# The second norm of a hybrid layer: early MLP weights split inside the output projection's sweep, and scaled stream differences

## The chip, the core and the metric

The kernel runs on one core of one Trainium2 chip. The metric is device time in microseconds (us) from the start to the end of one execution. The engines are named as in the profile: PE (TensorE, the matmuls), PEld (its weight loads), DVE (VectorE), ACT (ScalarE), POOL (GpSimd) and SP (SyncE, which issues the DMAs here).

## The reference, cut to what matters

One layer: a normed and modulated input goes through attention and gated linear attention, the two are merged, projected and added to `x`; then a second norm, a modulation and an MLP with a squared ReLU, added again. The change lies where the first residual becomes the second norm's input.

```
def rms_norm(x, g):
    y = x * lax.rsqrt(jnp.mean(x * x, axis=-1, keepdims=True) + EPS)
    return y * g
def modulate(h, shift, scale):
    return h * (1 + scale) + shift
def sq_relu_mlp(h, w1, w2):
    return jnp.square(jax.nn.relu(h @ w1)) @ w2
# in hybrid_layer
    x = x + gt1 * ((...) @ w_out)                       # branch_merge ends with w_out
    x = x + gt2 * sq_relu_mlp(modulate(rms_norm(x, norm2), sh2, sc2), w_mlp1, w_mlp2)
```

Sizes: 1024 tokens, `D_MODEL` 1024, `D_FF` 4096, all float32.

## The kernel before

The stream is kept transposed: 128 channels on the partitions, tokens along the free axis. `th` is a half of the tokens (512 columns), `c` a half of the channels. Every product is three matmuls (`mm3`, lines 163 to 165): the float32 operands are split into a high part (a cast on ACT) and a low part (a subtraction on DVE), and high x high, high x low and low x high are summed. A weight block is split by `split` (lines 1111 and 1112) into one of six buffers tagged `W`; an activation block by `split_block` (lines 1138 and 1139). A **product** below is one `product` call: twelve matmuls of 512 columns.

`out_projection` multiplies by `w_out`. For each `th` and `c` it loads two 1 MB weight tiles (`R`, two buffers), makes eight products into four PSUM banks, adds the residual on DVE (line 1300), stores the new stream to `x` in DRAM (line 1301, on SP's queue) and squares it on ACT (1306) to sum the squares on DVE (1307). After each `th` the sum goes over the partitions by eight small matmuls (line 350), a reciprocal root is made on DVE (lines 121 to 126), transposed to all partitions by PE (line 362) and copied by ACT (1328). Then every tile of the half is multiplied by the root (DVE 1333), and scaled and shifted on ACT (1334).

The MLP's first matrix is multiplied by a seven-product scheme: `unit(u)` makes a 1024 x 256 slice of it with seven products instead of eight, in the order `(0, 1, 5, 4, 6, 2, 3)`. Their right sides are blocks `B[i, j]`, four tiles `j` each: blocks 0 and 1 are the first token half, 5, 4, 6, 2 and 3 are sums and differences that need the second half. Their weights are, likewise, plain blocks (0, 1, 3) or sums that `sums` makes on POOL (lines 1159 to 1162) for 5, 4, 6 and 2. `sink` takes the products out of PSUM (lines 1379 to 1414), squares them and stores them to `u`. There are 16 units, run in pairs.

Since blocks 0 and 1 need the first half alone, units 0 to 3 run their products 0 and 1 (eight in all) behind the output projection, and `norm2_second` makes the other five blocks meanwhile: on DVE two multiplications by the root, two differences and five low parts for each of four tile pairs `j` (36 instructions), on POOL eight subtractions, on ACT the scale and shift and the casts. `mlp` then goes on with units 0 and 1.

The code gives an order of issue; a scheduler places the instructions of each engine by it and by its own estimate of time, and each engine runs its list in that order. `tc.issue_after` puts instructions behind another one. SP issues DMAs in order, and a DMA waits there until its buffer is free.

## Time and profile before

| | |
|---|---|
| time, median of 3 runs | 2125.89 us (2125.73 to 2126.91) |
| time of the profiled execution | 2125.22 us, of which the span of instructions 2123.5 us |
| PE busy | 2014.4 us (95%) |
| DVE busy | 1435.5 us (68%) |
| ACT busy | 1053.7 us (50%) |
| POOL busy | 677.7 us (32%) |
| mean granted TensorE clock | 0.984 of full speed |
| chain that ended last | PE 75%, DVE 11%, ACT 4%, DMA 4% |

An engine's busy time says how much work it has; where the time goes is read from the waits of PE, stretch by stretch, and from the instructions on the other engines that stand behind each wait.

### The profile page before, as it was taken

The page shows a single profiled execution, that of the slowest core. Times are in us where ns is not written, and L with a number is a line of the kernel's source. Part 1 is how long each engine was busy: PE and PEld are TensorE (multiplying, and loading weights), DVE is VectorE, ACT ScalarE, POOL GpSimd, SP SyncE. Part 2 cuts the span into 40 slices and gives each one's busy share as a digit, 9 for nine tenths or more (in the row PEclk, how much of TensorE's full clock was granted, in tenths as well). Part 3 has the DMA queues.
Part 4 walks back from the last instruction along what each step waited for, and adds up shares of the span by engine and source line. Part 5 has one row for each costly group of instructions (what it writes and reads, how often), then busy time and mean ns, then how long its engine had stood idle before and what let it go on. Part 6 is the DMA issues. An engine that isn't in the chain of part 4 may idle for free.

```text
span 2123.5 us, 32583 instructions
## 1 busy us (share of the span) xinstructions
PE 2014.4 (95%) x12526; PEld 1682.6 (79%) x12526; DVE 1435.5 (68%) x2088; ACT 1053.7 (50%) x1833; POOL 677.7 (32%) x436
## 2 busy tenths in 40 slices
PE   4999998999999999899999898999699999999999
PEld 2888777898889999677788686877588888788887
DVE  6533766749484387778777678857756457798794
ACT  3344655455553232687766543445555556344341
POOL 2100231322222022362301456103433235475470
PEclk9999999999999999999999999999899999999999
DMA  8234320212223333872311476744154547645441
GB/s 290 68 105 128 106 61 27 86 37 60 78 64 95 107 127 123 289 238 85 95 50 46 153 237 202 259 170 149 43 176 148 180 144 243 224 144 163 135 154 65
DMA packets 217339, 284.12 MB, mean 134 GB/s; under 512 B 18864, under 2 KB 139840, under 8 KB 217184
## 3 DMA queue, kind: packets, MB, share of 16 engines
q1 hardware_dynamic: 217120, 281.90, 40.6%
q8 instruction: 99, 1.62, 0.3%
q0 software_dynamic: 64, 0.13, 0.1%
q14 instruction: 56, 0.46, 0.1%
HBM read 200.18 MB, written 81.81 MB: 133 GB/s over the span
## 4 chain that ended last, share of the span: by engine, by line
PE 75%; DVE 11%; ACT 4%; DMA 4%; issue 3%; POOL 2%; SPq 1%; ACTq 0%; DVEq 0%; POOLq 0%
PE g L163 12%; PE g L165 12%; PE g L164 12%; PE p L165 8%; PE p L163 8%; PE p L164 7%; PE b L986 2%; PE a L713 1%; DVE G L863 1%; PE b L163 1%; PE b L165 1%; PE b L164 1%; PE s L163 1%; DMA S<-in_w_ada_dram 1%; PE a L715 1%
## 5 line engine op out<-in xcount | busy, mean ns | idle before, releaser
L163 PE MATMUL g<-whi,S 128*128 128x256 f32 x896 | 259.2, 289 | 0.0
L165 PE MATMUL g<-whi,S 128*128 128x256 f32 x896 | 251.2, 280 | 0.0
L164 PE MATMUL g<-wlo,S 128*128 128x256 f32 x896 | 250.5, 280 | 0.0
L1112 DVE TENSOR_TENSOR W<-Q,W 128x512 fp32r<-128x512 f32 x160 | 132.1, 830 | 103.6 <-ACT W L1111 103.1
L163 PE MATMUL p<-S,W 128*128 128x512 f32 x384 | 155.8, 406 | 22.6 <-ACT W L1111 19.0
L163 PEld LDWEIGHTS g<-whi,S 128*128 128x128 f32 x896 | 169.1, 189 | 1.8
L164 PEld LDWEIGHTS g<-wlo,S 128*128 128x128 f32 x896 | 169.1, 189 | 1.1
L165 PEld LDWEIGHTS g<-whi,S 128*128 128x128 f32 x896 | 169.1, 189 | 0.0
L1111 ACT CAST W<-R 128x512 fp32r<-128x512 f32 x152 | 93.9, 619 | 150.3 <-PE p L165 104.7
L1159 POOL TENSOR_TENSOR Q<-R 128x512 f32<-128x512 f32 x40 | 60.2, 1504 | 310.5 <-DVE W L1112 215.7
L163 PE MATMUL g<-S,whi 128*128 128x512 f32 x368 | 151.9, 413 | 5.8 <-ACT S L258 5.8
L165 PE MATMUL p<-S,W 128*128 128x512 f32 x384 | 155.4, 405 | 1.8 <-DVE W L1112 1.8
L151 POOL TENSOR_TENSOR wlo<-wraw,whi 128x1024 fp32r<-128x1024 f32 x32 | 81.8, 2571 | 234.7 <-ACT whi L150 218.9
L1112 DVE TENSOR_TENSOR W<-R,W 128x512 fp32r<-128x512 f32 x152 | 140.5, 926 | 21.8 <-ACT W L1111 21.8
L164 PE MATMUL p<-S,W 128*128 128x512 f32 x384 | 155.1, 404 | 0.0
L1111 ACT CAST W<-Q 128x512 fp32r<-128x512 f32 x160 | 98.4, 621 | 109.0 <-PE g L165 52.0
L164 PE MATMUL p<-G,W 128*128 128x512 f32 x384 | 152.0, 396 | 0.0
L165 PE MATMUL p<-G,W 128*128 128x512 f32 x384 | 151.9, 395 | 0.0
L163 PE MATMUL p<-G,W 128*128 128x512 f32 x384 | 151.9, 395 | 0.0
L164 PE MATMUL g<-S,whi 128*128 128x512 f32 x368 | 147.1, 400 | 0.0
L165 PE MATMUL g<-S,wlo 128*128 128x512 f32 x368 | 146.8, 399 | 0.0
L181 DVE TENSOR_TENSOR G<-b,G 128x512 fp32r<-128x512 f32 x160 | 108.9, 686 | 42.3 <-ACT G L180 41.7
(332 smaller groups left out, 5511.8 us busy)
## 6 DMA issues: line engine op xcount, KB each, us to landing
R<-in_w_mlp_dram SPq DMA_DIRECT2D x32, 1024.0 KB, 6.0
wraw<-in_w_in_dram SPq DMA_DIRECT2D x60, 512.0 KB, 3.9
u<-S SPq DMA_DIRECT2D x96, 256.0 KB, 2.3
S<-in_w_ada_dram SPq DMA_DIRECT2D x32, 512.0 KB, 5.9
G<-u SPq DMA_DIRECT2D x64, 256.0 KB, 3.6
S<-u SPq DMA_DIRECT2D x48, 256.0 KB, 3.5
G<-in_w_ada_dram SPq DMA_DIRECT2D x16, 512.0 KB, 10.6
R<-in_w_out_dram SPq DMA_DIRECT2D x8, 1024.0 KB, 6.2
```

The costliest lines, as they stand in the source:

```text
L151: self.lo_engine.tensor_tensor(lo[:, s, :], raw, hi[:, s, :].bitcast(F32), op=ALU.subtract)
L163: nc.tensor.matmul(out, lh, rh, start=first, stop=False, skip_group_check=more)
L164: nc.tensor.matmul(out, lh, rl, start=False, stop=False, skip_group_check=more)
L165: nc.tensor.matmul(out, ll, rh, start=False, stop=last, skip_group_check=more)
L181: self.nc.vector.tensor_tensor(lo, src, hi.bitcast(F32), op=ALU.subtract)
L713: nc.tensor.matmul(po, qd[:, s], sb, start=d == 1, stop=True)
L715: nc.tensor.matmul(pu, kd[:, s], vt(c), start=True, stop=True)
L863: nc.vector.tensor_tensor(uv[:, :, :, s, :], xv[:, :, :, 1 - s, :], tv[:, :, :, s, :], op=ALU.mult)
L986: nc.tensor.transpose(pt[:, h * P:(h + 1) * P], src, self.ident)
L1111: self.nc.scalar.copy(hi, v)
L1112: self.nc.vector.tensor_tensor(lo, v, hi.bitcast(F32), op=ALU.subtract)
L1159: tt(s[0], a21, a22, op=ALU.add)
```

## The change

The change rewrites what lies between the second half of the output projection (`th` = 1) and the MLP's units.

- Units 0 and 1 get their weights in the sweep: `early_weights` loads each unit's 1 MB in two tiles of the pool `S` (rows of 1 KB), before the sweep of `th` = 1 instead of behind it, and their `sums` on POOL are traced there. Units 2 and 3 get `half_weights`: 512 KB with rows of 512 B, for products 0 and 1 alone; their whole 1 MB is loaded again later. `ahead` splits six weight blocks between the last products of the projection: (unit 0, product 0), (1, 0), (0, 1), (1, 1), (2, 0), (3, 0).
- In the sweep ACT scales the even tiles of the stream in place by `mc[:, 2]` (line 1349), and DVE makes the scaled difference of odd and even tile, `t2` (line 1351), before the root is known. Behind the root a tile pair needs a multiplication and an addition for block 5, a multiplication and a scalar_tensor_tensor (STT) for block 4, and so on: with the low parts 44 instructions on DVE, none on POOL. The root is read from PSUM, without ACT's copy. The first half's even tiles get the shift's difference `dsh` added on ACT (four instructions) at the end of `norm2_first`.
- `norm2_second` yields after each block, and units 0 and 1 take their products in between.

```
@@ mm3, product
-        nc.tensor.matmul(out, ll, rh, start=False, stop=last, skip_group_check=more)
+        return nc.tensor.matmul(out, ll, rh, start=False, stop=last, skip_group_check=more)
+            if j == 1:
+                self.last_mm = r
@@ unit
+            if i == 5 and early is not None:
+                if "sums" in w:
+                    self.rest(blk, A, w, w.pop("sums"))
+                else:
+                    raw = self.raw_weights(src)
+                    self.rest(blk, A, w)
+                yield
...
+    def early_weights(self, u):
+        raw = [self.S(F32, (P, 4, 256)) for _ in range(2)]
+        for e in range(2):
+            self.nc.sync.dma_start(raw[e], self.wcols("w_mlp1", u * 256)[:, e::2, :])
+        return lambda kh, s: raw[kh][:, :, s * P:(s + 1) * P]
+    def half_weights(self, u):
+        raw = self.S(F32, (P, KT, P))
+        self.nc.sync.dma_start(raw, self.wcols("w_mlp1", u * 256)[:, :, 0:P])
+        return lambda kh, s: raw[:, kh::2, :]
@@ out_projection
+            if th == 1:
+                blk = [(self.half_weights if u > 1 else self.early_weights)(u) for u in range(4)]
+                early = [{"blk": blk[u], "sums": self.sums(blk[u])} for u in range(2)] + [{}, {}]
+                t2 = [self.S(F32, (P, 2, 512)) for _ in range(2)]
+                def ahead(u, i):
+                    early[u][i] = self.split(blk[u](i, 0))
...
+                    if th and c and kh:
+                        ahead(0, 0)
+                        ahead(1, 0)
...
+                        if th:
+                            j, e = b // 2, Z[1, 0, c][:, i // 2, :]
+                            if b % 2 == 0:
+                                nc.scalar.mul(e, e, mc[:, 2, b:b + 1])
+                            else:
+                                nc.vector.scalar_tensor_tensor(t2[c][:, i // 2, :], v, mc[:, 2, b:b + 1], e, op0=ALU.mult, op1=ALU.subtract)
+                        if th and c:
+                            ahead(*((0, 1), (1, 1), (2, 0), (3, 0))[i])
...
-        for u in (0, 1, 0, 1, 2, 3, 2, 3):
-            next(units[u])
-        self.norm2_second(rb, z)
+        rs, after = self.token_rstd(ssq)
+        next(units[0])
+        with self.tc.issue_after(after.ins):
+            next(units[1])
+        with self.tc.issue_after(self.last_mm.ins):
+            rp, _ = self.on_all(rs)
+        ahead(2, 1)
+        ahead(3, 1)
+        with self.tc.issue_after(after.ins):
+            next(units[0])
+        for u in (1, 2, 3, 2, 3, 0, 1):
+            next(units[u])
+        for _ in self.norm2_second(rp[0], z, lambda j: t2[j // 2][:, j % 2, :]):
+            for u in (0, 1):
+                next(units[u])
@@ norm2_second (new body)
+        for j in range(4):
+            tt(u(j), u(j), rb, op=ALU.mult)
+            tt(z(1, 1, j), u(j), z(0, 0, j), op=ALU.add)
+            self.block(5, j, z(1, 1, j))
+        yield
+        for j in range(4):
+            tt(z(1, 0, j), z(1, 0, j), rb, op=ALU.mult)
+            stt(z(0, 0, j), z(1, 0, j), sh(j), z(0, 0, j), op0=ALU.add, op1=ALU.subtract)
+            self.block(4, j, z(0, 0, j))
+        yield
+        for j in range(4):
+            b = self.B[6, j] = self.four(6)
+            nc.scalar.activation(b[:, 0, :], u(j), AF.Identity, bias=dsh(j))
+            stt(b[:, 1, :], u(j), dsh(j), b[:, 0, :].bitcast(F32), op0=ALU.add, op1=ALU.subtract)
+        yield
+        for j in range(4):
+            stt(u(j), u(j), sh(j), z(1, 0, j), op0=ALU.add, op1=ALU.add)
+            self.block(2, j, u(j))
+        yield
+        for j in range(4):
+            tt(u(j), z(0, 1, j), z(1, 1, j), op=ALU.subtract)
+        for j in range(4):
+            self.block(3, j, u(j))
+        yield
```

The order of the instructions, at three places. ACT at the end of the sweep, before: squares of the stream (`m<-G`) and casts of MLP weights (`W<-R`) alternate, and the last square (L1306) is followed by a copy out of PSUM.

```order
L1306 ACTIVATE m_14019<-G_13910 128x512 [waits DVE_49,Activation_49]
L1111 CAST W_14157<-R_14109 128x512 [waits PE_49,Activation_49]
L1306 ACTIVATE m_14039<-G_13908 128x512 [waits DVE_49,Activation_49]
L1111 CAST W_14178<-R_14109 128x512 [waits PE_49]
L1306 ACTIVATE m_14059<-G_13910 128x512 [waits DVE_49,Activation_49]
L1391 COPY S_14107<-p_14094 128x512 [waits PE_49]
L1111 CAST W_14187<-R_14185 128x512 [waits DMAHW4_49]
L1328 COPY m_14087<-a_14082 128x512 [waits PE_49,Activation_49]
```

ACT there now: before the last square (L1343, fourth from the end) stand two scalings of the stream in place (L1349) and three weight casts, one of them of the projection's last block (`W_14094`).

```order
L1343 ACTIVATE m_14039<-G_13942 128x512 [waits DVE_49]
L1111 CAST W_14091<-S_13770 128x512 [waits DMAHW0_49,PE_49,Activation_49]
L1349 ACTIVATE G_13942<-G_13942,mc 128x512 [waits DMAHW7_49,Activation_49]
L1343 ACTIVATE m_14063<-G_13944 128x512 [waits DVE_49]
L1111 CAST W_14094<-R_14014 128x512 [waits PE_49]
L1343 ACTIVATE m_14087<-G_13942 128x512 [waits DVE_49]
L1349 ACTIVATE G_13942<-G_13942,mc 128x512 [waits DMAHW1_49,Activation_49]
L1111 CAST W_14115<-S_13772 128x512 [waits DVE_49,PE_49]
L1343 ACTIVATE m_14111<-G_13944 128x512 [waits DVE_49]
L1453 COPY S_14151<-p_14138 128x512 [waits PE_49]
```

Two of these instructions wait for a DMA (`DMAHW`): the scalings, until the store of the unscaled tile has left. The last square now stands behind them.

PE, at the last product of unit 0 (product 3, into `p_14094`), before: it stands behind both units' product 2 (`g_14428` is unit 1's) and waits for nothing there.

```order
L163 MATMUL g_14428<-G_14356,W_14505 128x512
L164 MATMUL g_14428<-G_14356,W_14505 128x512
L165 MATMUL g_14428<-G_14356,W_14505 128x512
L163 MATMUL p_14094<-G_14363,W_14150 128x512
L164 MATMUL p_14094<-G_14363,W_14150 128x512
L165 MATMUL p_14094<-G_14363,W_14150 128x512
L163 MATMUL p_14094<-G_14366,W_14150 128x512
```

PE there now (unit 0's product 3 goes into `p_14138`, `p_14213` is unit 2's product 5, `g_14376` unit 1's product 2):

```order
L163 MATMUL p_14138<-G_14509,W_14277 128x512 [waits Activation_49]
L164 MATMUL p_14138<-G_14509,W_14277 128x512 [waits DVE_49]
L165 MATMUL p_14138<-G_14509,W_14277 128x512
L163 MATMUL p_14138<-G_14512,W_14277 128x512 [waits Activation_49]
L163 MATMUL p_14213<-S_14285,W_14577 128x512 [waits Activation_49]
L164 MATMUL p_14138<-G_14512,W_14277 128x512 [waits DVE_49]
L165 MATMUL p_14138<-G_14512,W_14277 128x512
L163 MATMUL p_14138<-G_14515,W_14277 128x512
L164 MATMUL p_14138<-G_14515,W_14277 128x512 [waits DVE_49]
L163 MATMUL g_14376<-G_14442,W_14481 128x512 [waits Activation_49]
```

Unit 0's product 3 moved ahead of unit 1's product 2, waits for casts and low parts tile by tile, and one matmul of unit 2, whose weights are POOL's sum, stands within it.

DVE at the end of the norm's work, before: the four low parts of block 3 (`G_14363` to `G_14372`), then the weight splits of units 0 and 1.

```order
L1139 TENSOR_TENSOR G_14363<-S_14281,G_14363 128x512 [waits Activation_49]
L1139 TENSOR_TENSOR G_14366<-S_14281,G_14366 128x512 [waits Activation_49]
L1139 TENSOR_TENSOR G_14369<-S_14282,G_14369 128x512 [waits Activation_49]
L1139 TENSOR_TENSOR G_14372<-S_14282,G_14372 128x512 [waits Activation_49]
L1112 TENSOR_TENSOR W_14375<-Q_14145,W_14375 128x512
L1112 TENSOR_TENSOR W_14391<-Q_14173,W_14391 128x512
L1112 TENSOR_TENSOR W_14407<-Q_14145,W_14407 128x512 [waits PE_49,Activation_49]
L1112 TENSOR_TENSOR W_14425<-Q_14173,W_14425 128x512 [waits PE_49,Activation_49]
```

DVE there now: a weight split of each of units 0 and 1 (`W_14457`, `W_14481`: product 2), four differences (L1424) and the low parts of block 3.

```order
L1441 TENSOR_TENSOR S_14371<-S_14371,p_14138 128x512 [waits PE_49,Pool_49]
L1112 TENSOR_TENSOR W_14457<-Q_13774,W_14457 128x512
L1141 TENSOR_TENSOR G_14454<-S_13785,G_14454 128x512 [waits Activation_49]
L1112 TENSOR_TENSOR W_14481<-Q_13779,W_14481 128x512
L1424 TENSOR_TENSOR S_13784<-G_13386,G_13788 128x512 x2
L1424 TENSOR_TENSOR S_13785<-G_13538,G_13944 128x512
L1424 TENSOR_TENSOR S_13785<-G_13538,G_13944 128x512 [waits DVE_49]
L1141 TENSOR_TENSOR G_14509<-S_13784,G_14509 128x512 [waits Activation_49]
L1441 TENSOR_TENSOR S_14151<-S_14151,g_14358 128x512 [waits PE_49]
L1141 TENSOR_TENSOR G_14512<-S_13784,G_14512 128x512 [waits Activation_49]
L1141 TENSOR_TENSOR G_14515<-S_13785,G_14515 128x512 [waits Activation_49]
L1141 TENSOR_TENSOR G_14518<-S_13785,G_14518 128x512 [waits Activation_49]
```

The weights' splits came ahead of block 3's work. POOL's first sum for unit 2 waits for the cast and the split of `W_14457`, and DVE's rows from there on run beside POOL's eight sums for units 2 and 3.

## Rows read from the trace of the kernel before

**Rows 1.** What PE waited for, 1380 to 1580 us: total, times, longest, us.
```profile
PE p L163 <- ACT W L1111: 15.6, 2, 14.4
PE p L165 <- DVE W L1112: 1.8, 1, 1.8
```
**Rows 2.** PE in order of time: start us, us, instruction, idle time before.
```profile
1466.29 1.02 PE L350 MATMUL a<-ones,m 128*128 128x1 f32 x8 [0.19 <-DVE m L1307]
...
1470.36 0.62 PE L362 MATMUL a<-ident,ty 128*128 128x128 f32 x4
...
1489.41 0.50 PE L163 MATMUL p<-S,W 128*128 128x512 f32 x1 [1.17 <-ACT W L1111]
...
1504.55 0.80 PE L163 MATMUL p<-S,W 128*128 128x512 f32 x1 [14.40 <-ACT W L1111]
...
1514.72 0.40 PE L163 MATMUL g<-G,W 128*128 128x512 f32 x1
...
1559.52 0.40 PE L163 MATMUL p<-G,W 128*128 128x512 f32 x1
```
**Rows 3.** Stretches: us, busy of PE, PEld, DVE, ACT, POOL, granted clock, DMA, GB/s.
```profile
1488.24:1514.72 26.48, 9.09 (x25) 6.48 (x25) 20.59 (x25) 13.52 (x25) 8.91 (x6) 0.61 0.05 20
1514.72:1559.52 44.80, 44.80 (x193) 36.07 (x192) 27.03 (x32) 23.78 (x41) 24.03 (x16) 1.00 0.39 130
1660.00:1760.00 100.00, 100.00 (x431) 80.49 (x430) 54.31 (x72) 54.30 (x93) 35.49 (x24) 1.00 0.43 145
```
**Rows 4.** DVE in order of time, from the sweep's end to the root.
```profile
1463.94 0.74 DVE L1300 SCALAR_TENSOR_TENSOR G<-p,mc,G 128x512 f32<-128x512 f32 x1
...
1465.45 0.69 DVE L1307 TENSOR_TENSOR m<-m,m 128x512 f32<-128x512 f32 x1 [0.16 <-ACT m L1306]
...
1470.05 0.17 DVE L126 SCALAR_TENSOR_TENSOR ty<-ty,ty 128x4 f32<-128x4 f32 x1
```
**Rows 5.** DMA issues of the whole run: count, KB each, median us to landing.
```profile
R<-in_w_mlp_dram SPq DMA_DIRECT2D x32, 1024.0 KB, 6.0
wraw<-in_w_in_dram SPq DMA_DIRECT2D x16, 256.0 KB, 3.3
```
**Rows 6.** The stores of the stream to `x`, 1380 to 1480 us.
```profile
DMA to landing us min/median/max: 2.1/3.7/6.3
```
**Rows 7.** SP in order of time: the last weight tile of the projection.
```profile
1432.81 0.38 SPq L1104 DMA_DIRECT2D R<-in_w_out_dram  x1
```
**Rows 8.** ACT in order of time, behind the first half's norm.
```profile
1432.91 1.52 ACT L1334 ACTIVATE G<-G,mc 128x512 f32<-128x512 f32 x2
...
1435.90 1.65 ACT L1111 CAST W<-R 128x512 fp32r<-128x512 f32 x3
```
**Rows 9.** DVE and POOL in order of time, where both work (POOL rows last).
```profile
1485.68 1.28 DVE L1353 TENSOR_TENSOR S<-G,G 128x512 f32<-128x512 f32 x2
...
1489.77 1.75 DVE L1353 TENSOR_TENSOR S<-G,G 128x512 f32<-128x512 f32 x1
1491.45 1.75 DVE L1352 TENSOR_TENSOR G<-G,G 128x512 f32<-128x512 f32 x1
1493.12 0.67 DVE L1379 TENSOR_TENSOR S<-S,g 128x512 f32<-128x512 f32 x1
...
1485.32 3.97 POOL L1358 TENSOR_TENSOR G<-G,G 128x512 f32<-128x512 f32 x1 [4.33 <-DVE G L1352]
1489.26 3.39 POOL L1363 TENSOR_TENSOR S<-G,S 128x512 f32<-128x512 f32 x2
...
1524.74 1.29 POOL L1159 TENSOR_TENSOR Q<-R 128x512 f32<-128x512 f32 x1 [23.77 <-DVE W L1112]
```
**Rows 10.** PE at another wait, in order of time.
```profile
120.14 0.64 PE L491 MATMUL a<-ident,G 128*128 128x128 f32 x2 [3.42 <-DVE G L486]
```
**Rows 11.** The stretch behind that wait; columns as in rows 3.
```profile
120.00:124.00 4.00, 3.86 (x20) 3.89 (x21) 2.65 (x3) 1.79 (x3) 0.00 (x0) 0.57 0.64 204
```

More of the change, by code (lines that the diff above doesn't have):

```diff
@@ L1121, in product @@
             c, b = j * P, x(j)
-            self.mm3(out, w[:, 0, c:c + P], w[:, 1, c:c + P], b[:, 0, :], b[:, 1, :], first and j == 0, last and j == 3, more and not first)
+            r = self.mm3(out, w[:, 0, c:c + P], w[:, 1, c:c + P], b[:, 0, :], b[:, 1, :], first and j == 0, last and j == 3, more and not first)
+            if j == 1:
+                self.last_mm = r
     ORDER = (0, 1, 5, 4, 6, 2, 3)
@@ L1163, in sums, with unit @@
         return s
-    def unit(self, src, sink, halves=True):
+    def unit(self, src, sink, halves=True, early=None):
         B = self.B
-        raw = self.raw_weights(src)
-        blk = (lambda kh, s: raw[:, kh::2, s * P:(s + 1) * P]) if halves else (lambda kh, s: raw[:, 4 * kh:4 * kh + 4, s * P:(s + 1) * P])
-        A, w, bank = {0: blk(0, 0), 1: blk(1, 0)}, {}, {}
+        raw = None if early else self.raw_weights(src)
+        blk = early.pop("blk") if early and "blk" in early else (lambda kh, s: raw[:, kh::2, s * P:(s + 1) * P]) if halves else (lambda kh, s: raw[:, 4 * kh:4 * kh + 4, s * P:(s + 1) * P])
+        A, w, bank = {} if early else {0: blk(0, 0), 1: blk(1, 0)}, early or {}, {}
         for i in self.ORDER:
+            if i == 5 and early is not None:
[5 more added lines that the diff above has]
+                yield
             wi = w.pop(i) if i in w else self.split(A[i])
@@ L1177, in unit, with rest @@
             self.product(p, wi, lambda j: B[i, j], i in (0, 1, 4), True)
-            if i == 1:
-                A[4], A[5], A[6], A[2] = self.sums(blk)
-                w[3] = self.split(blk(1, 1))
+            if i == 1 and early is None:
+                self.rest(blk, A, w)
             sink(i, p)
             yield
+    def rest(self, blk, A, w, sums=None):
+        A[4], A[5], A[6], A[2] = sums or self.sums(blk)
+        w[3] = self.split(blk(1, 1))
+    def early_weights(self, u):
[7 more added lines that the diff above has]
+        return lambda kh, s: raw[:, kh::2, :]
     def pair(self, a, b, also=None):
@@ L1275, in load_mod @@
         nc.vector.scalar_tensor_tensor(mc[:, 2, :], mc[:, 2, :], 1.0, vec[:, V_N2:V_N2 + 8], op0=ALU.add, op1=ALU.mult)
+        self.dsh = self.cp.tile([P, 4], F32, name="dsh")
+        nc.vector.tensor_tensor(self.dsh, mc[:, 1, 1::2], mc[:, 1, 0::2], op=ALU.subtract)
     def out_projection(self):
@@ L1307, in out_projection @@
                             nc.vector.tensor_tensor(ssq, ssq, sq, op=ALU.add)
+                        if th:
[6 more added lines that the diff above has]
+                            ahead(*((0, 1), (1, 1), (2, 0), (3, 0))[i])
             z = lambda t, e, j: Z[t, e, j // 2][:, j % 2, :]
-            rb = self.norm2_scale(ssq)
             if th == 0:
+                rs, _ = self.token_rstd(ssq)
+                rp, _ = self.on_all(rs)
+                rb = self.m()
+                nc.scalar.copy(rb, rp[0])
                 self.norm2_first(rb, z)
-        self.units = units = [self.mlp1_unit(u) for u in range(16)]
-        for u in (0, 1, 0, 1, 2, 3, 2, 3):
+        self.units = units = [self.mlp1_unit(u, early[u] if u < 4 else None) for u in range(16)]
+        rs, after = self.token_rstd(ssq)
[3 more added lines that the diff above has]
+        with self.tc.issue_after(self.last_mm.ins):
+            rp, _ = self.on_all(rs)
+        ahead(2, 1)
[3 more added lines that the diff above has]
+        for u in (1, 2, 3, 2, 3, 0, 1):
             next(units[u])
-        self.norm2_second(rb, z)
+        for _ in self.norm2_second(rp[0], z, lambda j: t2[j // 2][:, j % 2, :]):
+            for u in (0, 1):
+                next(units[u])
     def block(self, i, j, v, engine=None):
@@ L1415, in sink @@
                 put(3, x3)
-        return self.unit(self.wcols("w_mlp1", u * 256), sink)
+        return self.unit(self.wcols("w_mlp1", u * 256), sink, early=early)
     def mlp2_unit(self, n, q, x):
@@ L1435, in mlp @@
         units = self.units
-        for u in (0, 2):
-            for _ in range(5):
-                next(units[u])
-                next(units[u + 1])
+        for _ in range(6):
+            next(units[2])
+            next(units[3])
         for u in range(4, 14, 2):
```

28 lines of the change are left out of this document (6 added, 22 removed).

## Prediction

> **What bounds the kernel now.** I read the page first: PE is busy 95% of the span and makes up 75% of the chain that ended last, so only what PE waits for is worth time. Then PE's waits around the second norm [rows 1]: one of 14.4 us, two smaller, all put down to weight splits (L1111, L1112). PE in order of time [rows 2] shows the place. The eight products that units 0 to 3 can make from the first token half end at 1488.24 (1489.41 less its idle 1.17). The next products run at speed only from 1514.72 on. From there to 1559.52, where unit 2 begins its last product, stand 192 matmuls: 44.80 / 192 = 0.2333 us each, at full clock [rows 3]. From 1488.24 to 1559.52 there are 24 more, 216 in all: 216 x 0.2333 = 50.4 us of work in 71.3 us. **20.9 us are lost**, and they are all this place has to give. In that hole DVE is busy 20.6 us of 26.5 and the granted clock means 0.61 [rows 3]: the named split is late because DVE and ACT are still making blocks for the second token half in front of it. Afterwards PE has no hole in 100 us stretches such as 1660 to 1760 [rows 3], so what is won here stays won.
>
> **The sweep, where work is added.** The projection's last product ends ten matmuls before L350 [rows 2], at 1463.6, and each product before it took 12 x 0.2333 = 2.8 us. SP issues the projection's last weight tile at 1432.81 [rows 7]; the order puts six loads of 512 KB directly behind it, and the stores of the stream behind those. A 1 MB load takes 6.0 us to landing, a 256 KB one (512 B rows, like units 2 and 3) 3.3 us [rows 5]: 6.0, two of 6.0 and four of 3.3 make 31 us one after the other, landed at 1464. Each has a start that the next one hides; I take half, 1448. Unit 2's weights are first split two products before the end, at 1458: cover 10 us, and at 1464 PE would wait some 3 us. POOL's eight sums for units 0 and 1 ran beside the sweep before, too.
>
> ACT gets four additions at the end of `norm2_first`: 4 x 0.76 [rows 8], 3.0 us in front of the next four weight casts. Those started at 1435.90 [rows 8], now about 1439.5, and PE needs the first eight products before the end, at 1441.2: free, with under 1 us of cover; uncovered it costs what exceeds that.
>
> At the sweep's end things come closer. PE's order puts seven matmuls of unit 0 into the last product, five of them before its end: 5 x 0.2333 = 1.2 us. Behind it DVE adds the residual (0.74), ACT squares (0.63), and DVE has a weight split, a t2 difference and only then the sum of squares: 0.6 + 0.7 + 0.7. Before, the addition began at 1463.94 and the sum ended at 1466.14 [rows 4]; now 1465.0 + 0.7 + 0.7 + 0.6 + 0.7 = 1467.7. So L350 starts at 1467.7 instead of 1466.29 [rows 2]. The scaling that stands before the last square on ACT waits for the store of tile 6, issued at about 1461.7: with the shortest landing, 2.1 us, it is not seen, with the median, 3.7 [rows 6], it adds 1 us. I take none, as the queue is empty by then; the ends are 0 and 2 us. Between L350 and the ninth product PE now has 84 matmuls (before, 86): 19.6 us, and 1.9 for the small matmuls of the root as before (21.95 - 86 x 0.2333). The ninth product can start at 1467.7 + 19.6 + 1.9 = 1489.2, **1.0 us later** than 1488.24.
>
> **Behind the root.** ACT's copy of the root goes, and POOL's eight subtractions; DVE has 44 instructions instead of 36, besides splits and sinks. The root is on all partitions at about 1472.2 (twelve matmuls behind L350, then L362's 0.62). To the low part of block 5's first tile DVE has 20 instructions, to its fourth 24. DVE starts SBUF instructions back to back every 0.60 to 0.64 us (two took 1.28 [rows 9]) and STTs every 0.7 (0.74 [rows 4]): 24 x 0.61 = 14.6, with half a microsecond of waits for ACT 1487.3. PE wants it nine matmuls into the ninth product, 1491.3: **no wait, 4.0 us of cover**; each microsecond beyond that is lost. So the 14.4 and 1.2 us waits go, and with them the slow clock. What is late next? To the split of unit 0's product 2, the last DVE instruction before POOL starts again, DVE has 50 instructions, 12 of them STTs: 38 x 0.605 + 12 x 0.66 + 1.2 of waits = 32.1, so 1504.3. PE begins that product at 1506.0 and, without a wait in its seven products, ends it at 1489.2 + 84 x 0.2333 = 1508.8.
>
> **The new wait.** There PE meets unit 0's last product, whose right side, block 3, DVE has not begun; in PE's order it now stands before unit 1's product 2, and one matmul of unit 2 is inside it. Just then POOL, released by that split, starts eight sums for units 2 and 3, and DVE has 19 instructions to the low part of unit 2's weights, 16 of them with both inputs in SBUF. Where both engines run such instructions at once, both slow down: DVE 1.75 and 1.75 with a start every 1.68 us, POOL 3.39 for two, while alone they take 0.6 and 1.29 [rows 9]. One that reads PSUM keeps its 0.67 [rows 9]. So eight pairs at 1.68 = 13.4, eight single ones 4.8, three from PSUM 1.8: 20.1 us, to 1524.4. PE wants that part 37 matmuls behind 1508.8, at 1517.4. By block 3's low parts (the first is the sixth of the pairs, 1515.0, the third about 1518.9) and the 28 matmuls behind the third PE gets there at 1525.4. I take 1525.4: **8.0 us lost**. Bounds: below, POOL does not get in (one of its instructions took 3.97 us beside a dense DVE [rows 9]): 1.5 us; above, the pairs and a DVE 2 us late: 10.5. A wait of some 6 us also lowers the clock: after a wait of 3.42 us [rows 10] the next 4 us had a mean of 0.57 [rows 11], mostly the lower of the two levels, 1.2 GHz. If 3.5 us run at half speed, 1.7 are lost, part of it behind DVE's own lateness: **1.0**, ends 0 and 2.
>
> The Trainium skill, SBUF — State Buffer, section "SBUF: two separate sides", speaks against putting these together: DVE with two SBUF inputs and POOL take a common port pair in turn, each for its whole instruction. By that rule a pair would cost 0.69 + 1.29 = 1.98 and the stretch 2.4 us more; the rows say 1.68, and the rows decide.
>
> **Sum.** 20.9 - 1.0 - 8.0 - 1.0 = 10.9 us. The profiled execution took 2125.22 us, its span 2123.5; this gives 2114.3, and, as the median is 0.67 above it, **2115.0**.
>
> **Rivals.** (1) DVE keeps the port, or POOL's sums fit beside it: 1.5 instead of 9.0 lost, gain 18.4, **2107.5**, 2106 with nothing lost. For it: two DVE instructions in 1.28 us while POOL's one took 3.97 [rows 9]. Against: the 19 instructions include three PSUM reads and several waits for ACT, where POOL gets in, and unit 2's weights need POOL's third sum in any case. (2) The chain behind the root is slower than counted, say 0.69 per instruction instead of 0.62: 50 x 0.07 = 3.5 us, plus 2 us by a late store before the last square; block 5 is then just late, and the whole train with it: gain 5.4, **2120.5**. For it: DVE, ACT and PE hand to each other some twenty times in that chain. (3) Slower: the six loads. On ACT the projection's last split stands behind unit 2's weights, so PE stops at 1461.7, four matmuls into the last product's time, until they land, and every microsecond behind that is lost; from landing at 1472.6 on the forecast's gain is gone. That needs over 40 us for 4 MB, where one after the other gives 31. With 1480 the time is **2133**. (4) The wait only moves: block 3 comes 9 us later than counted, as POOL's sums and DVE's splits for both units 2 and 3 end before PE goes on: **2124**.
>
> **How the numbers follow.** Forecast (gain 8 to 14) 0.58, rival 1 0.17, rival 2 0.15, rival 3 0.06, rival 4 0.04. 2115.0 is the likeliest. The range goes from rival 1's 2106.5 to 2121.5, past rival 2; left out is about 0.12. A measurement here tells 0.2% (4.3 us) from no change: faster 0.90, same 0.04, slower 0.06.
>
> **What would show it.** Right: PE without a wait from 1489 to 1509; then waits for DVE of some 8 us in two or three pieces at products into `p` (units 0 to 2), DVE instructions of 1.7 us beside POOL's sums, a granted clock near 0.6 for some us. L350 at 1467 to 1469. Wrong at the first step: a wait at L163 or L165 before 1467 put down to ACT's L1111 or a DMA. Wrong at the second: a wait at the ninth product. Wrong at the third: no wait at unit 0's last product (rival 1). A gain beyond 20.9 us is not explained by anything here.

## The result, and the profile after

| | before | after |
|---|---|---|
| time, median | 2126.4 us (2125.73 to 2127.75, 4 runs) | 2100.53 us (2094.93 to 2101.94, 4 runs) |
| ratio to before | | 0.9875 (0.9863 to 0.9887) |
| profiled execution, of which its span | 2125.22 us, 2123.5 us | 2101.28 us, 2099.3 us |
| mean granted TensorE clock | 0.984 | 0.982 |

The kernel became 25.9 us faster. 2115.0 had been forecast, with a range from 2106.5 to 2121.5: the sign was right, the size was not, and the result lies below the range. More was gained than the 20.9 us that PE lost at the second norm before.

At the second norm the waits changed much as forecast. PE's waits there, 1380 to 1600 us (total, times, longest, as in [rows 1]):

```profile
PE p L163 <- ACT W L1111: 4.2, 1, 4.2
PE p L165 <- DVE W L1112: 1.3, 2, 0.8
PE a L350 <- DVE m L1344: 1.2, 1, 1.2
PE p L164 <- DVE G L1141: 0.3, 1, 0.3
```

The 14.4 us wait of [rows 1] is gone; one of 4.2 us has come. PE in order of time, as in [rows 2], shows where it stands:

```profile
1470.00 1.02 PE L350 MATMUL a<-ones,m 128*128 128x1 f32 x8 [1.21 <-DVE m L1344]
...
1492.09 0.39 PE L163 MATMUL p<-S,W 128*128 128x512 f32 x1
...
1511.77 0.50 PE L164 MATMUL p<-G,W 128*128 128x512 f32 x1 [0.25 <-DVE G L1141]
...
1516.90 0.80 PE L163 MATMUL p<-S,W 128*128 128x512 f32 x1 [4.16 <-ACT W L1111]
```

The ninth product begins at 1492.09 without a wait; the new wait is the one matmul of unit 2 that PE's order puts into unit 0's last product.

The rest of the gain is in no wait. The stretch 1660 to 1760, where PE never idles, in the columns of [rows 3] (what stands in brackets behind PE is its number of matmuls):

```profile
1660.00:1760.00 100.00, 100.00 (x443) 82.81 (x442) 56.54 (x78) 56.69 (x98) 29.23 (x21) 1.00 0.58 192
```

Before, the same 100 us at the same granted clock of 1.00 held 431 matmuls [rows 3]; now they hold 443. The code of these units is the same. Two pairs of rows, twelve matmuls apart, give the spacing. PE before, at 512 columns in the MLP and at 256 columns in the projections of the first half of the run (start, duration):

```profile
1699.99 0.40 PE L165 MATMUL g<-G,W 128*128 128x512 f32 x1
...
1702.79 0.40 PE L165 MATMUL g<-G,W 128*128 128x512 f32 x1
...
799.73 0.28 PE L165 MATMUL g<-whi,S 128*128 128x256 f32 x1
...
801.13 0.28 PE L165 MATMUL g<-whi,S 128*128 128x256 f32 x1
```

PE after, the same two places:

```profile
1699.89 0.39 PE L165 MATMUL g<-G,W 128*128 128x512 f32 x1
...
1702.61 0.39 PE L165 MATMUL p<-G,W 128*128 128x512 f32 x1
...
799.79 0.28 PE L165 MATMUL g<-whi,S 128*128 128x256 f32 x1
...
801.23 0.28 PE L165 MATMUL g<-whi,S 128*128 128x256 f32 x1
```

At 512 columns 2.80 / 12 = 0.2333 us became 2.72 / 12 = 0.2267; at 256 columns 1.40 / 12 = 0.1167 became 1.44 / 12 = 0.1200. Matmuls all over the run changed their pace, in parts of the program that the diff does not touch, the long ones for the better and the short ones for the worse. There are about 3,700 of 512 columns with split weights (`W`) in each trace, which by estimate gives 3,700 x 0.0066 = 24 us.

What can reach all of them is where the tiles lie. The change adds one small tile, `dsh` (16 bytes a partition), ahead of the activation tiles; the memory map of the program as built shows it taking 32 bytes, so that all activation tiles (`S`, `G` and those behind them) start 32 bytes further on. The weight tiles (`whi`, `wlo`, `W`, `R`) are laid out from the other end and stayed.

### The profile page after: what moved, and what is told of

Its sections match the earlier page's. It is cut to its first block, busy times and chain, and to the rows that moved or that the text cites. A ratio compares the mean times of both kernels' runs of the same rounds, so it can differ in the third digit from the quotient of the medians.

```text
span 2099.3 us, 32592 instructions
## 1 busy us (share of the span) xinstructions
PE 2001.9 (95%) x12526; PEld 1696.1 (81%) x12526; DVE 1436.3 (68%) x2101; ACT 1052.3 (50%) x1832; POOL 668.8 (32%) x428
## 4 chain that ended last, share of the span: by engine, by line
PE 76%; DVE 8%; ACT 5%; DMA 5%; issue 3%; POOL 2%; SPq 1%; ACTq 0%; DVEq 0%; POOLq 0%
PE g L163 13%; PE g L165 13%; PE g L164 13%; PE p L163 7%; PE p L165 7%; PE p L164 7%; PE b L986 2%; PE a L713 1%; DMA S<-in_w_ada_dram 1%; PE b L163 1%; PE b L165 1%; PE b L164 1%; PE a L715 1%; PE s L163 1%; DMA wraw<-in_w_in_dram 1%
## 5 line engine op out<-in xcount | busy, mean ns | idle before, releaser
L163 PE MATMUL g<-whi,S 128*128 128x256 f32 x896 | 262.4, 293 | 0.0
L165 PE MATMUL g<-whi,S 128*128 128x256 f32 x896 | 254.7, 284 | 0.0
L1112 DVE TENSOR_TENSOR W<-Q,W 128x512 fp32r<-128x512 f32 x160 | 129.3, 813 | 88.6 <-ACT W L1111 88.5
L163 PEld LDWEIGHTS g<-whi,S 128*128 128x128 f32 x896 | 172.5, 192 | 1.8
L165 PEld LDWEIGHTS g<-whi,S 128*128 128x128 f32 x896 | 172.5, 193 | 0.0
L163 PE MATMUL p<-S,W 128*128 128x512 f32 x384 | 153.7, 400 | 11.3 <-ACT W L1111 7.8
L1111 ACT CAST W<-R 128x512 fp32r<-128x512 f32 x142 | 87.9, 621 | 132.0 <-PE p L165 93.4
L165 PE MATMUL p<-S,W 128*128 128x512 f32 x384 | 152.6, 397 | 0.0
L164 PE MATMUL p<-S,W 128*128 128x512 f32 x384 | 152.4, 397 | 0.0
L165 PE MATMUL p<-G,W 128*128 128x512 f32 x384 | 149.9, 390 | 1.3 <-DVE W L1112 1.3
L164 PE MATMUL p<-G,W 128*128 128x512 f32 x384 | 150.2, 391 | 0.3 <-DVE G L1141 0.3
L163 PE MATMUL p<-G,W 128*128 128x512 f32 x384 | 149.7, 390 | 0.0
L1112 DVE TENSOR_TENSOR W<-R,W 128x512 fp32r<-128x512 f32 x142 | 128.3, 904 | 10.1 <-ACT W L1111 10.1
```

The lines of the kernel that those rows point to most:

```text
L163: nc.tensor.matmul(out, lh, rh, start=first, stop=False, skip_group_check=more)
L164: nc.tensor.matmul(out, lh, rl, start=False, stop=False, skip_group_check=more)
L165: return nc.tensor.matmul(out, ll, rh, start=False, stop=last, skip_group_check=more)
L1111: self.nc.scalar.copy(hi, v)
L1112: self.nc.vector.tensor_tensor(lo, v, hi.bitcast(F32), op=ALU.subtract)
```

## The experiments

### Placement against order: two kernels that separate them

`b_s32` is the kernel before with activations moved as the change moves them, `a_s0` the changed kernel with activations at their places modulo 64 bytes of before. Both edit one line, the tile `mc` that lies ahead of the activations (rows it has beyond the fourth are not used):

```
-        self.mc = mc = self.cp.tile([P, 4, KT], F32, name="mc")
+        self.mc = mc = self.cp.tile([P, 5, KT], F32, name="mc")
```

> The kernel before, with one change: the small tile of modulation vectors that is allocated ahead of the activation pools is 32 bytes per partition longer, so that all activation tiles (S, G and those behind them) lie 32 bytes further on, as they do in the changed kernel. Instructions and their order stay. Theory P (placement: the changed kernel gained most of its unforecast time because its activations moved by 32 bytes, and 512-column matmuls then start every 0.2267 us instead of 0.2333): 2113 us, between 2109 and 2117, with 0.2267 in the trace (3700 matmuls against split weights x 0.0066 is 24 us, less what the 256-column ones lose, up to 9, and what other engines hide). Theory R (all of the gain comes from the rewritten second norm): 2126, with 0.2333.

> The changed kernel with the same tile 32 bytes longer, so that activation tiles lie at multiples of 64 bytes again, as before the change. Order and instructions are those of the changed kernel. Theory P: 2114 us (2111 to 2118), 512-column matmuls every 0.2333 us; what is left of the gain, some 11 to 12 us, is the rewritten norm's. Theory R: 2100.5.

Measured: `b_s32` 2110.33 us (2108.71 to 2113.18, ratio 0.9926, 0.9909 to 0.9944), `a_s0` 2115.77 us (2115.17 to 2117.37, ratio 0.9952, 0.9936 to 0.9967), the kernel before beside them 2125.85. The stretch 1660 to 1760 of `b_s32`:

```profile
1660.00:1760.00 100.00, 100.00 (x443) 82.84 (x442) 56.51 (x77) 55.78 (x96) 34.10 (x23) 1.00 0.52 174
```

and of `a_s0`:

```profile
1660.00:1760.00 100.00, 100.00 (x430) 80.33 (x429) 56.57 (x76) 54.92 (x94) 33.02 (x23) 1.00 0.50 169
```

The old order at the new place has the new pace, the new order at the old distance has the old pace. **Theory R falls.** Placement alone gives 2125.85 - 2110.33 = 15.5 us, the order alone 2125.85 - 2115.77 = 10.1, together 25.6, against 25.9 measured for both. With 3,700 matmuls gaining 24 us, why only 15.5? `b_s32` reaches the second half's L350 just 1 us earlier than before (1465.32 against 1466.29), since its 256-column matmuls lose what the others win in the first part of the run. Behind L350 stand 2,678 of the 3,700, some 17.7 us by the same estimate, of which 14.7 arrive in the profiled span: a later wait for a weight split grew from 3.6 to 5.1 us, and the granted clock behind it was 0.50 for 6.8 us instead of 3.4.

### Which places count

Two kernels move the weights, `a_w0` alone and `a_s0w0` together with the line of `a_s0`, by an unused tile of 32 bytes ahead of the weight tiles:

```
+        self.rp, close_rp = self.open("rp", side="right")
+        self.rp.tile([P, 8], F32, name="rpad", bufs=1)
         self.wts, self.close_wts = self.open("wts", side="right")
```

> The changed kernel with the weight tiles (whi, wlo, W, R) 32 bytes lower, at multiples of 64, and the activations left where the change put them (32 bytes behind a multiple of 64). Tells two forms of theory P apart. P1, only the distance between moving and stationary operand counts (equal places modulo 64: 0.2267, unequal: 0.2333): 2114 us. P2, each operand's own place counts (a moving one 32 behind a multiple of 64 is quick, a stationary one on a multiple of 64 is quick): 0.2267 or below, 2100 or below. Theory R: 2100.5.

> The changed kernel with activations and weights all on multiples of 64 bytes. P1 (the distance counts): 0.2267 us per matmul and 2100 us. P2 (each operand's own place): 0.2333 or a little less, 2112 to 2116. Theory R: 2100.5.

Measured: `a_w0` 2115.85 us (2113.89 to 2120.03), as slow as `a_s0`, so not the activations' own place but its relation to the weights counts; `a_s0w0` 2096.37 us (2093.94 to 2106.29), as P1 said to within its spread. Yet its spacing was not that of the changed kernel: 0.2289 us at 512 columns and 0.1143 at 256. So "equal modulo 64" was not the whole rule, and the next kernel, `mc` with 8 rows, broke it:

> The changed kernel with the tile ahead of the activation pools 128 bytes longer: the activations' place modulo 64 and modulo 128 is that of the changed kernel, only modulo 256 it differs from the weights'. Theory 64 (only places modulo 64 count): 512-column matmuls every 0.2267 us, 256-column ones every 0.120, 2100 us. Theory far (a larger distance counts too; with 64 bytes between the two, in a_s0w0, the starts were 0.2289 and 0.1143 us apart): 256-column matmuls at 0.117 or less, and 2096 or less.

Measured: 2116.56 us (2110.17 to 2118.28), 0.2325 and 0.1189. Equal places modulo 64 and 128 do not help: **theory 64 falls**, and what `far` expected of a larger distance falls with it. Four kernels, run once each, then tested the distance itself (`b_w0`: the three lines above in the kernel before; the others: `mc` with 20, 12 and 18 rows):

> The kernel before with its weight tiles (whi, wlo, W, R) 32 bytes lower and the activations where they were. The distance from a weight tile to an activation tile becomes the one of the changed kernel (256 bytes modulo 512), while both now lie on multiples of 64. Theory D (the distance alone decides): 512-column matmuls every 0.2267 us and 256-column ones every 0.120, 2110 us (2107 to 2114), as b_s32. Theory O (each operand's own place decides, so that this is like a_s0w0): 0.2289 and 0.1143, 2106 or less.

> The changed kernel with activations 512 bytes further on. Theory D with a period of 512 bytes (a slice of 128 weights is 512 bytes of a row): 0.2267 and 0.120 us as in the changed kernel, 2100 us. Without such a period: another value, 0.2289 to 0.2333, 2108 to 2116.

> The changed kernel with activations 256 bytes further on, the point farthest from the changed kernel's distance modulo 512. If a 512-column matmul only gets slower away from that distance (32 bytes: 0.2333, 64: 0.2289, 128: 0.2325): 0.2325 to 0.2335, 2113 to 2117. If the pattern repeats every 256 bytes: 0.2267, 2100.

> The changed kernel with activations 448 bytes further on, which is 64 bytes below the changed kernel's distance modulo 512, where a_s0w0 is 64 above. If the effect is even about that distance: 0.2289 us and 0.114 to 0.117 us at 256 columns, 2096 us. If it is not: 0.2325 to 0.2335, 2112 to 2116.

All kernels together, from each program's memory map (bytes from a weight tile to an activation tile, modulo 256), with the mean spacing of consecutive matmuls at full clock in each trace (some 3,600 at 512 columns with `W`, some 2,600 at 256 columns with `whi` or `wlo`). Of a matmul's two operands the one that PEld loads is called stationary, the one whose columns are counted moving.

| kernel | distance | 512 columns, us | 256 columns, us | time, us |
|---|---|---|---|---|
| before | 224 | 0.2333 | 0.1170 | 2125.9 |
| `b_s32` | 0 | 0.2268 | 0.1198 | 2110.3 |
| `b_w0` (one run) | 0 | 0.2268 | 0.1198 | 2110.1 |
| after | 0 | 0.2268 | 0.1198 | 2100.5 |
| `a_s256` (one run) | 0 | 0.2268 | 0.1198 | 2100.6 |
| `a_s512` (one run) | 0 | 0.2268 | 0.1198 | 2098.6 |
| `a_s0`, `a_w0` | 32 | 0.2333 | 0.1183 | 2115.8, 2115.9 |
| `a_s0w0` | 64 | 0.2289 | 0.1143 | 2096.4 |
| `a_s128` | 128 | 0.2325 | 0.1189 | 2116.6 |
| `a_s448` (one run) | 192 | 0.2333 | 0.1175 | 2119.2 |

The stretch 1660 to 1760 of two of them shows the two ends of it. `a_s256`:

```profile
1660.00:1760.00 100.00, 100.00 (x443) 82.83 (x442) 56.54 (x77) 57.28 (x99) 29.06 (x21) 1.00 0.59 194
```

`a_s448`:

```profile
1660.00:1760.00 100.00, 100.00 (x431) 80.55 (x430) 56.39 (x76) 55.21 (x94) 35.40 (x24) 1.00 0.48 160
```

`b_w0` and `b_s32` lie at different absolute places with the same distance and have the same pace: **theory D holds, the distance decides**, theory O falls. `a_s256` repeats the changed kernel, so the pattern returns every 256 bytes, sooner than the 512 that D named. `a_s448`, 64 below a multiple of 256, is slow where `a_s0w0`, 64 above, is middling: the pattern is not even. In all distances tried 512 columns run best at a multiple of 256, and 256 columns (where the tiles' roles are exchanged: weights move and activations are stationary) best at 64 above. Why a distance matters to PE at all, whether by its two readers meeting in the memory, was not tried and stays open.

### What is left of the wait: POOL's sums beside DVE's block 3

In `a_s0`, with the pace of before, the predicted wait can be read undisturbed. The two longest of PE's waits there, 1380 to 1600 us:

```profile
PE p L164 <- DVE G L1141: 3.9, 1, 3.9
PE p L163 <- ACT G L1140: 2.4, 1, 2.4
```

and POOL's first sum for unit 2 with DVE's four differences and first low part of block 3 (POOL and DVE in order of time):

```profile
1508.20 1.63 POOL L1161 TENSOR_TENSOR Q<-R 128x512 f32<-128x512 f32 x1 [53.07 <-ACT S L1442]
...
1510.29 6.80 DVE L1424 TENSOR_TENSOR S<-G,G 128x512 f32<-128x512 f32 x4
1517.02 1.75 DVE L1141 TENSOR_TENSOR G<-S,G 128x512 fp32r<-128x512 f32 x1
```

POOL and DVE alternate, 6.80 / 4 = 1.70 us each, and block 3 is late. In the changed kernel the same work went the other way (POOL, DVE and ACT in order of time):

```profile
1507.64 5.22 POOL L1161 TENSOR_TENSOR Q<-R 128x512 f32<-128x512 f32 x1 [51.59 <-ACT S L1442]
1512.82 1.71 POOL L1163 TENSOR_TENSOR Q<-R 128x512 f32<-128x512 f32 x1
1514.49 1.70 POOL L1162 TENSOR_TENSOR Q<-Q,R 128x512 f32<-128x512 f32 x1
...
1508.63 2.49 DVE L1424 TENSOR_TENSOR S<-G,G 128x512 f32<-128x512 f32 x4
1511.04 0.68 DVE L1141 TENSOR_TENSOR G<-S,G 128x512 fp32r<-128x512 f32 x1
1511.64 0.68 DVE L1441 TENSOR_TENSOR S<-S,g 128x512 f32<-128x512 f32 x1
1512.23 4.51 DVE L1141 TENSOR_TENSOR G<-S,G 128x512 fp32r<-128x512 f32 x3
...
1516.23 0.62 ACT L1111 CAST W<-Q 128x512 fp32r<-128x512 f32 x1 [3.94 <-POOL Q L1162]
```

DVE runs its four differences in 2.49 us, POOL's first sum takes 5.22 instead of 1.29 and ends soon after DVE turns to an instruction that reads PSUM (L1441, 1511.64). Block 3 is in time, and now POOL's third sum, cast by ACT at 1516.23, is what PE waits for. Either way PE stands still for 4 to 6 us. The Trainium skill, SBUF — State Buffer, section "SBUF: two separate sides", calls the shared pair an exclusive lock rather than a split of bandwidth; the row of 5.22 us agrees, and adds that a dense DVE stream can keep it over several instructions. The pairs of 1.70 us in `a_s0` are shorter than 0.69 + 1.29 = 1.98 us, both instructions alone one after the other, as an exclusive lock would have them; there the rows decide.

Which of the two wins was not settled, but two causes can be ruled out. Eleven traces have this stretch in the changed kernel's order on POOL and DVE. In six POOL's first sum is kept out for 5.2 us (after, `a_again`, `a_s512`, `a_w0`, `a_s0w0`, `c_pe`), in five it is not and DVE's differences take 6.8 us (`a_s0`, `a_s128`, `a_s256`, `a_s448`, `pe_s0w0`). It is not the distance between tiles: `a_s256` has that of the changed kernel, and its rows (POOL, then DVE) are those of `a_s0`.

```profile
1504.62 1.62 POOL L1161 TENSOR_TENSOR Q<-R 128x512 f32<-128x512 f32 x1 [52.30 <-ACT S L1442]
1506.71 6.79 DVE L1424 TENSOR_TENSOR S<-G,G 128x512 f32<-128x512 f32 x4
```

Nor is it the moment at which POOL comes: in all eleven its first sum starts 0.22 us behind the same DVE instruction (L1141; 1504.40 in `a_s256`, 1507.42 in after).

Two kernels moved the pieces. `c_pe` puts unit 2's first matmul behind unit 1's last product:

```
+        with self.tc.issue_after(self.last_mm.ins):
+            next(units[2])
```

> The changed kernel (same placement of tiles) with one thing moved: on PE the first matmul of unit 2's product 5 no longer stands inside unit 0's product 3 but behind unit 1's. Theory C (POOL's sums for units 2 and 3 and DVE's block 3 take turns at the SBUF port; the wait of 4.16 us at that matmul is POOL's third sum): the wait at unit 2's matmul goes, but the low parts of block 3 are still late beside POOL's sums, so that PE waits 3 to 4 us at unit 0's product 3 instead, in two or three pieces: 2097 to 2101. Rival (the wait is only that matmul's place in PE's order, and DVE is in time): all of the 4.2 us and the 2.4 us of low clock behind it come back: 2094.

Measured: 2097.61 us (2096.64 to 2098.76), within theory C's range and above its rival's 2094; the 2.9 us to the changed kernel (2094.93 to 2101.94) lie within the spread. The two longest of PE's waits there, 1420 to 1600 us:

```profile
PE g L163 <- ACT S L1460: 2.3, 1, 2.3
PE p L164 <- DVE G L1141: 1.7, 3, 0.7
```

The wait for unit 2's weights is gone, and block 3's low parts cost 1.7 us in three pieces instead; the 2.3 us are new, ACT's copy out of PSUM being queued behind the cast that waits for POOL's sum. `c_both` also holds POOL's sums back until block 3 is done (`dsh8` is `dsh` with four more columns):

```
+        hold = nc.gpsimd.tensor_copy(self.dsh8[:, 4:5], self.B[3, 3][:, 1, 0:1].bitcast(F32))
+        with self.tc.issue_after(hold.ins):
+            next(units[2])
+            next(units[3])
```

> As c_pe, and POOL's eight sums for units 2 and 3 are held back by a one-element copy on POOL that reads the last low part of block 3, so that DVE has the four differences and the low parts behind it alone. Theory C: the four differences take 2.5 us, no DVE row of 1.7 us before the last low part, PE passes units 0 and 1 without a wait, and the sums (some 1.3 to 1.7 us each) are in time for unit 2: 6 us faster than the changed kernel, 2094 (2092 to 2097). Rival (the sums are late whatever DVE does): the wait moves to unit 2's first matmul with 4 us or more, 2099 to 2103.

Measured: 2100.84 us (2093.84 to 2105.09). The median misses theory C's range and lies in its rival's, with a wait of 3.66 us where the rival had 4 or more; the fastest execution is within C's, so the time alone decides nothing. DVE, POOL and PE in order of time (L1425 is the differences' line here):

```profile
1506.40 2.49 DVE L1425 TENSOR_TENSOR S<-G,G 128x512 f32<-128x512 f32 x4
...
1510.01 1.89 DVE L1141 TENSOR_TENSOR G<-S,G 128x512 fp32r<-128x512 f32 x3
...
1520.65 3.43 DVE L1112 TENSOR_TENSOR W<-Q,W 128x512 fp32r<-128x512 f32 x2
...
1513.36 1.74 POOL L1163 TENSOR_TENSOR Q<-R 128x512 f32<-128x512 f32 x1
...
1522.45 0.79 PE L165 MATMUL p<-S,W 128*128 128x512 f32 x1 [3.66 <-DVE W L1112]
```

Block 3 is made at DVE's full speed, as C said, but the sums then run beside DVE's next work, and unit 2's low weights (L1112 at 1520.65) are late: 3.66 us. Holding POOL back chose another product to pay.

### Which half of the change earned its 10 us

`d_oldnorm` keeps the early weights and takes the blocks' old recipe (no scaling and no difference in the sweep, the old body of `norm2_second` with a yield behind each block). `d_late` keeps the new recipe and loads and splits the weights of units 0 to 3 behind the sweep.

```
# d_oldnorm, norm2_second behind the root
+            norm(0, j)
+            norm(1, j)
+            tt(z(0, 0, j), z(1, 0, j), z(0, 0, j), op=ALU.subtract)
+            tt(T2(j), z(1, 1, j), z(0, 0, j), op=ALU.subtract)
+            self.block(5, j, T2(j))
# d_late
-        self.units = units = [self.mlp1_unit(u, early[u] if u < 4 else None) for u in range(16)]
+        self.units = units = [self.mlp1_unit(u) for u in range(16)]
```

> Half of the change: the early weights and the order of units stay as changed, while the blocks behind the root are made as before (scale and shift on ACT, two products with the root and two differences per tile pair on DVE, eight subtractions on POOL, the root copied by ACT; no scaling and no difference in the sweep). Theory N (the shorter chain behind the root is what makes block 5 ready in time): PE stops at block 5 again, for DVE has three instructions and waits for ACT twice per tile pair before its low part: 6 to 10 us slower than the changed kernel, 2107 to 2111. Theory W (the split weights were the whole wait): within 3 us of it, 2098 to 2103.

> The other half: the new chain behind the root with the scaling and the differences in the sweep, while the weights of units 0 to 3 are loaded and split behind the sweep as before. Theory N: block 5 is early, but the weight splits for products 5 stand behind norm work on DVE and POOL's sums are made beside it: half of the hole remains, 2104 to 2108. Theory W: PE waits nearly as long as before, 2108 to 2112 (the kernel before, with its activations 32 bytes further on, took 2110.3).

Both halves keep the new order of the units, so "early weights" below stands for weights and order together.

Measured: `d_oldnorm` 2098.21 us (2096.66 to 2101.18), `d_late` 2104.52 us (2102.03 to 2106.94), both at the distance of the changed kernel, where the old order takes 2110.3. The time of `d_oldnorm` is theory W's, that of `d_late` theory N's, and PE stops at block 5 in `d_oldnorm` as theory N says: neither theory is right alone. PE's waits in it, 1420 to 1600 us:

```profile
PE p L165 <- DVE W L1112: 4.8, 1, 4.8
PE p L164 <- DVE S L1141: 1.2, 1, 1.2
PE a L350 <- DVE m L1344: 0.7, 1, 0.7
PE p L163 <- ACT W L1111: 0.4, 1, 0.4
```

Without the new recipe PE waits 6.4 us in three pieces at the ninth and tenth products: 1.2 us for a low part of block 5, and 5.2 for weight splits, which DVE and ACT make among the norm's work. But its later products then find everything ready, and its sweep is shorter: from the first half's L350 to the second's 46.8 us, against 49.0 in the changed kernel, whose scalings and differences in the sweep make the projection's own weight splits late (0.8 and 0.4 us) and delay the last sum. In `d_late`, with POOL's sums for units 0 and 1 beside the end of the sweep, two sums and a difference on DVE take 1.77 or 1.78 us each, and the sum of squares is 3.4 us late:

```profile
1469.03 1.34 PE L350 MATMUL a<-ones,m 128*128 128x1 f32 x8 [3.42 <-DVE m L1336]
```

So the early weights alone earn all of it (12.1 us from `b_s32`). The shorter chain behind the root is worth 5.8 us when it comes alone (`b_s32` to `d_late`) and adds nothing measurable to them: `d_oldnorm` took 2096.7 to 2101.2, the changed kernel 2094.9 to 2101.9. The traces say the same with less spread, from the first half's L350 to the end of the span: two of the changed kernel take 678.4 and 678.3 us there (after, `a_again`), though their spans differ by 3.9, and `a_s512` and `a_s256`, of the same order and distance, 680.0 and 680.8; `b_s32` takes 688.1, `d_late` 682.6 and `d_oldnorm` 676.5.

### The changed kernel again, and two combinations

`old_s0w0` and `pe_s0w0` are `d_oldnorm` and `c_pe` at the distance of `a_s0w0`.

> The changed kernel as it is, once more, on the chip of the next three. All theories: 2100 us (2095 to 2103), with a wait of 4 us at unit 2's matmul within unit 0's product 3 or, as in a_s0, two waits at block 3.

> d_oldnorm (early weights, blocks behind the root made as before the change) with activations and weights placed as in a_s0w0. If placement and order add up as they did so far (a_s0w0 against the changed kernel: -4 us; d_oldnorm against it: -2): 2094 us (2091 to 2097). If the shorter chain of the changed kernel is worth something once 256-column matmuls are quicker: 2097 to 2100.

> c_pe (the changed kernel with unit 2's first matmul behind unit 1's product 3) with activations and weights placed as in a_s0w0. If placement and order add up: 2093.5 us (2091 to 2096), the fastest of all. If not, as a_s0w0: 2096 to 2098.

Measured: `a_again` 2100.27 us (2097.38 to 2101.99), `old_s0w0` 2100.70 (2091.89 to 2102.85), `pe_s0w0` 2095.79 (2091.41 to 2096.12, ratio to before 0.9858, 0.9839 to 0.9877). `a_again` waits 4.17 us at unit 2's matmul, as the changed kernel did. `pe_s0w0` is the fastest of all by its median, 4.5 us under the changed kernel beside it, but only 0.6 under `a_s0w0`, whose distance it has: it did not add up (2093.5 was expected). In its trace POOL gets in beside DVE, and PE waits 2.6 and 3.9 us at block 3, where the moved matmul has nothing to save. `old_s0w0` gained nothing over `d_oldnorm` and misses both of its ranges by its median. Single executions of one kernel differ by up to 12 us here, so differences of 2 or 3 us between their times are not claimed.

## Why the prediction was wrong, step by step

- **The step that failed: the pace of PE was taken as given.** "44.80 / 192 = 0.2333 us each" is measured well [rows 3], but it is a property of the program's memory map, not of a 512-column matmul: 0.2267 was possible. The prediction costed `dsh` as four additions on ACT and did not ask where that tile lies. In the runs it became 0.2267 with a tile of 16 bytes ahead of the activations. That is 15.5 us of the 25.9 (`b_s32`), and it explains why no case reached the result. The sentence "they are all this place has to give" was true of the place and wrong as a bound on the kernel; the last sentence, that a gain beyond 20.9 us is not explained, was the right alarm.
- **The order's own gain: right in sum, by two errors that partly cancel.** 10.9 us were forecast. With the old pace kept (`a_s0`) it is 10.1 us by the medians, 2115.77 us against the forecast of 2115.0; with the new pace (`b_s32` to after) 9.8. Of its terms the lateness of the ninth product was put too low (1.0 us, in `a_s0` 3.2) and the new wait with its low clock a little too high (9.0, in `a_s0` 8.3), both below. That the sum came so near is in part luck.
- **The loads: in time, between the two values counted.** Landing was taken at 1448, and put at 1464 with the loads one after the other. The six loads were issued from 1434.7 to 1440.2, and took in the trace of after, from issue to landing (the trace has it for five of them):

```profile
DMA to landing us min/median/max: 7.5/9.4/11.5
```

  The last one landed at 1451.7, 3.7 us later than taken and 12 before 1464: they overlap. PE waited for none of them, and rival 3 did not come.
- **The sweep's end: the chain was right, its start was not.** From the last residual addition to the end of the sum 2.6 us passed (2.7 forecast), and the store's landing was not seen, as taken. But L350 came late. Places in time of two executions can't be compared to a microsecond (the first half's L350 stands at 1421.0 in after and at 1417.2 in `a_again`), so the sweep is measured from that one. PE before, then after:

```profile
1419.51 1.02 PE L350 MATMUL a<-ones,m 128*128 128x1 f32 x8
...
1420.98 1.02 PE L350 MATMUL a<-ones,m 128*128 128x1 f32 x8
```

  With 1466.29 and 1470.00 for the second half's, the sweep took 46.8 us before and 49.0 after (49.0 in `a_again`, 49.4 in `a_s0`); 48.2 were forecast. The projection's own splits, behind scalings on ACT and differences on DVE, cost waits of 0.8 and 0.4 us that the working did not have. And behind PE's wait of 1.2 us at L350 the granted clock fell, in after and in `a_s0`, though not in `a_again` (after's stretch, in the columns of [rows 3]):

```profile
1471.00:1474.00 3.00, 3.00 (x9) 2.35 (x9) 1.96 (x12) 0.00 (x0) 0.00 (x0) 0.50 0.00 0
```

  Counted from the first half's L350, the ninth product was ready to begin at 68.7 us before, at 71.1 after and at 71.9 in `a_s0`: 2.4 and 3.2 us later, where 1.0 was forecast.
- **Block 5: right.** No wait at the ninth product; its last low part ended at 1491.1, and PE wanted it nine matmuls into the product, 1494.1: 3.0 us of cover, 4.0 forecast.
- **The new wait: right in place and nearly in size, right in cause where POOL gets in.** 8.0 us at unit 0's last product, and 1.0 of low clock, were forecast. In `a_s0` it is 6.2 us in two waits (2.35 and 3.88) and 2.1 more for ten matmuls at a lower clock, 8.3 in all; in the changed kernel 4.4, and 2.6 for twelve such matmuls, 7.0. So in `a_s0` block 3 is late as forecast, while in the changed kernel POOL's third sum is. The low clock was put at less than half its price. The stretch behind the wait in the changed kernel, in the columns of [rows 3]:

```profile
1516.90:1522.00 5.10, 5.10 (x12) 4.04 (x13) 4.12 (x4) 2.74 (x5) 5.10 (x4) 0.50 0.28 104
```

  A granted clock of 0.50 is the 1.2 GHz level: 5.1 us at it, where the working took 3.5.
- **Rival 1 was half true.** DVE kept the port in the changed kernel, as the row of 3.97 us in [rows 9] allowed, but that made no rival of it: POOL's third sum was late instead, the objection that the prediction itself raised. Rivals 2 and 4 did not come: block 5 was in time, and no wait of 9 us more appeared.
- **The rival that was missing** is that PE itself runs at another pace because tiles move. The profile of before could not have priced it, since all its matmuls with `W` stand at one distance; the diff could have raised the question, and a wide bound.

## What to carry to other kernels

When a change adds, drops or resizes any tile, compare the memory maps before pricing anything else: a 16-byte tile moved every tile behind it and was worth more than the reordering it came with. Count PE's matmuls in a stretch of the same work without waits in both kernels; if the number differs at the same granted clock, no wait explains it, and a padded copy of the kernel before is the control. And where two engines take turns at something, moving work between them may only choose who is late, as it did in `c_pe` and `c_both`; less work in that stretch, or more cover, was not tried here.

## What the runs showed of the hardware that was not expected

- Matmuls of 512 float32 columns started every 0.2267, 0.2289, 0.2325 or 0.2333 us at a granted clock of 1.00, by the distance between moving and stationary tile modulo 256 bytes; those of 256 columns every 0.1143 to 0.1198 us, with the best distance another one.
- With activations 0, 256 and 512 bytes further on than in the changed kernel the spacing was the same; 32 bytes either way made it 2.9% longer at 512 columns.
- A POOL instruction of 1.29 us took 5.22 us beside a dense stream of DVE instructions with two SBUF inputs, and in other traces of the same work the two alternated at 1.70 us, although POOL's instruction started 0.22 us behind the same DVE instruction in all of them.
